# A hybrid token mixer on one Trainium2 core: the upper weight part times both token parts in one 512-column matmul

## The chip, the core and the metric

The kernel runs on one core of one Trainium2 chip. Its engines work side by side, each on its own queue of instructions in program order: PE (TensorE, matmuls and transposes), DVE (VectorE), ACT (ScalarE), POOL (GpSimd), and SP (SyncE), which here issues most DMAs. The metric is the device time of one execution in microseconds, lower is better.

## What is computed

A block of 256 tokens behind 16 learned meta tokens (272 columns) is normalised and multiplied with one wide matrix `w_in` (2048 x 18568); three recurrent mixers (A: HGRN2, B: mLSTM, C: RWKV-7) work on slices of that product; their outputs are multiplied with `w_br`, gated, summed, multiplied with `w_out`, added to the input and normalised.

```python
xn = rmsnorm(h, norm_g[l])                       # h: 16 meta tokens, then x
(a_q, a_f, a_i, a_z, b_q, b_k, b_v, b_o, b_ig, b_fg, b_z,
 c_r, c_k, c_v, c_wd, c_ad, c_z, g_a, g_b, g_c) = split_cols(xn @ w_in[l])
y_a = hgrn2_mixer(a_q, a_f, a_i, a_z, ...)
y_b = mlstm_mixer(b_q, b_k, b_v, b_o, b_ig, b_fg, b_z, ...)
y_c = rwkv7_mixer(c_r, c_k, c_v, c_wd, c_ad, c_z, ...)
merged = (jax.nn.sigmoid(g_a) * (y_a @ w_br[l, 0])
          + jax.nn.sigmoid(g_b) * (y_b @ w_br[l, 1])
          + jax.nn.sigmoid(g_c) * (y_c @ w_br[l, 2]))
h = h + merged @ w_out[l]
return rmsnorm(h, final_norm_g)[:, N_META:]
```

All of it is float32. What matters for the change is `xn @ w_in`, and that the outputs `a_q`, `a_z`, `b_o`, `b_z` and `c_z` are needed for the 256 real tokens alone.

## The kernel before, in words

**Products in two parts.** A float32 product is made of three faster ones. Tokens and weights are each cut into an upper part (rounded to the format `F32R`) and a lower part (what the rounding left): `xH`, `xL`, and `wh`, `wl`. The product is `wh*xH + wh*xL + wl*xH`, all summed in one PSUM bank. The tokens are cut once at the start. The weights come by DMA in units of 4 row tiles x 256 columns (or 2 x 512) into `raw` (four buffers); ACT casts a unit to `wh`, DVE subtracts to get `wl` (three buffers each; class `Stream`, lines 334 to 375).

**Blocks.** `proj` (line 405) enters one block per 256 output columns of `w_in`; `gemm` (line 392) runs it: 16 row tiles x 2 halves `j` of 128 output channels x 3 products, 96 matmuls, each with weights as the stationary operand and 256 to 272 token columns streaming (`unit`, line 379). When a block's 96 matmuls are done, an evacuation function works on each `j`: tanh on ACT and a multiply on DVE (`silu2_evac`, line 409), tanh alone (`o_evac`, line 957), and others. PSUM has four banks `gp` for blocks, and a block uses two of them.

**Order.** Blocks run as C0 (K, V, Z), B0 (Q, K, V, O, Z, V, O, Z), C1, B1, C2, A0, A1, C3, A2, A3 (a digit is a group; C has four groups of R, K, V, Z; A has four of F, Q, I, Z). Beside them run the recurrent parts, `c_scan` (line 508), `b_scan` and `a_scan` (line 1140), as generators. A planner (class `Order`) keeps a clock of its own for PE, ACT and DVE, charges every instruction a price, and after each half unit starts the scan steps that its clock finds ready; the tile framework then arranges the instructions of each engine by its own estimate of when they become ready. Where a scan has small matmuls, they lie between the block's big ones.

**The C scan.** Each `c_scan` ends in a serial part of five chunks (line 733). A chunk is a round trip of PE, DVE and ACT, three times: matmul `cbank<-UV,SC`, copies to `cX`; matmul `cbank<-cX,Vm`, copies to `UV`; matmul `cbank<-UV,BT`, the new state `cS`, copies to `UV` for the next chunk. Before the chunks come 31 steps of a triangular inverse on DVE (`Ltmp` and `LV`, line 657), a copy `LT`, DMAs through DRAM into `Vm` and `VT`, and the matmuls `cbank<-VT,SC` and `cbank<-Vm,ZT`.

**After the projections** (line 1367): for B, then C, then A, four blocks of gate columns of `w_in` alternate with four blocks of `w_br`, 512 columns wide. Here the tokens are stationary and the weights stream: `gp<-wh,xH` and so on, 96 matmuls per gate block, then 48 of `gp<-wh,yHB` and its kind. `yHB` and `yLB` are the two parts of B's output, cut in `split` (line 1371). They lie in the pool `late`, which `l_setup` (line 1342) opens after closing the pool of `c_scan`; the two share memory.

```python
    def l_setup():
        od.finish(cst["prev"]["scan"])
        cst["ctx"].close()
        lp = ctx.enter_context(tc.tile_pool(name="late", bufs=1, side="right"))
```

Of the kernel before, what the change touches and what calls it, by code (L numbers as in the profile page):

```python
# [10 lines left out]
F32R = mybir.dt.float32r  # L11
# [3 lines left out]
ALU = mybir.AluOpType  # L15
AX = mybir.AxisListType

P = 128
D = 2048
KT = D // P  # L20
NMETA = 16
SEQ = 256
T = NMETA + SEQ
UK = 4
# [126 lines left out]
def kernel(  # L151
# [29 lines left out]
    od = Order()  # L181
    V = Priced(nc.vector, "dve", od, tc)
    S = Priced(nc.scalar, "act", od, tc)

    def mm(o, lhsT, rhs, start, stop):
        nc.tensor.matmul(o, lhsT, rhs, start=start, stop=stop)  # L186
        n = 1
        for d in rhs.shape[1:]:
            n *= d
        od.cost("pe", max(n, 256) / 2400 + 0.003 if lhsT.dtype == F32R else max(4 * n / 2400, 0.04 if lhsT.shape[1] <= 32 else 0.1))  # L190
# [10 lines left out]
    xnp = ctx.enter_context(tc.tile_pool(name="xnp", bufs=1))  # L201
# [19 lines left out]
    def wx(shape, name, dt=F32):  # L221
        return ev.tile(shape, dt, name=name, tag="wx", bufs=6)
# [111 lines left out]
    class Stream:  # L334
# [5 lines left out]
        def add(self, src, kts):  # L340
            uk = min(UK, 1024 // src.shape[2])
            for u in range(kts // uk):
                self.todo.append(src[:, u * uk:(u + 1) * uk, :])
# [33 lines left out]
    ws = Stream()  # L377

    def unit(h, l, u, kts, ps, aH, aL, t0, n, js):
        for k in range(UK):  # L380
            kk = u * UK + k
            rh = aH[:, kk, t0:t0 + n]
            mm(ps, h[:, k, js], rh, start=kk == 0, stop=False)
            mm(ps, h[:, k, js], aL[:, kk, t0:t0 + n], start=False, stop=False)
            mm(ps, l[:, k, js], rh, start=False, stop=kk == kts - 1)

    def apart(f):
        saved, od.ready = od.ready, od.clk["pe"]
        f()
        od.ready = saved  # L390

    def gemm(m, aH, aL, kts, t0, n, evac):
        nt = m // P
        ps = [gps.tile([P, 512], F32, name="gp", tag="g") for _ in range(nt)]
        for u in range(kts // UK):
            h, l = ws.next()
            for j in range(nt):
                unit(h, l, u, kts, ps[j][:, 0:n], aH, aL, t0, n, slice(j * P, (j + 1) * P))
                od.pump()
        for j in range(nt):  # L400
            apart(lambda: evac(j, ps[j][:, 0:n]))

    blocks = []

    def proj(c0, m, t0, evac, before=None, after=None):
        ws_src = win[:, :, c0:c0 + m]
        blocks.append((ws_src, KT, lambda: gemm(m, xH, xL, KT, t0, T - t0, evac), before, after))

    def silu2_evac(dst, off=0):
        def f(j, ps):  # L410
            n = ps.shape[-1]
            o = dst()[:, j, off:off + n]
            S.activation(out=o, in_=ps, func=AF.Tanh, scale=0.5)
            V.scalar_tensor_tensor(out=o, in0=o, scalar=1.0, in1=ps, op0=ALU.add, op1=ALU.mult)
        return f

    def copy_evac(dst):
        def f(j, ps):
            S.copy(out=dst()[:, j, :], in_=ps)
        return f  # L420

    xH = xnp.tile([P, KT, T], F32R, name="xH", tag="xa")
    xL = xnp.tile([P, KT, T], F32R, name="xL", tag="xb")
    WDH = [const.tile([P, T], F32R, name=f"WDH{i}") for i in range(2)]
    WDL = [const.tile([P, T], F32R, name=f"WDL{i}") for i in range(2)]

# [33 lines left out]
    def c_group(g):  # L460
# [23 lines left out]
        if g == 0:  # L484
            alloc()
        else:
            proj(C_R + c0, 256, NMETA - 2, sh("R", 0, NMETA - 2), before=lambda: (od.finish(prev["scan"]), alloc(),
                                                          nc.gpsimd.memset(st["R"][:, :, 0:NMETA - 2], 0.0)))
        proj(C_K + c0, 256, 0, sh("K", 8))
        proj(C_V + c0, 256, 0, sh("V", 16), after=begin)  # L490
        proj(C_Z + c0, 256, NMETA, silu2_evac(lambda: st["Z"]), before=zalloc, after=zdone)
        cst["prev"] = st
        return st
# [431 lines left out]
    def b_group(g):  # L925
        st = {}
        T0 = NMETA - 4

        def alloc():
            if bst.get("last"):  # L930
                od.finish(bst["last"])
            st["Q"] = ev.tile([P, 2, T], F32, name="bQ", tag="x1")
            st["K"] = ev.tile([P, 2, T], F32, name="bK", tag="x2")

        proj(B_Q + 256 * g, 256, T0, conv_evac(lambda: st["Q"], 2 * g, T0), before=alloc)
        proj(B_K + 256 * g, 256, 0, conv_evac(lambda: st["K"], 4 + 2 * g, 0))
        for hh in range(2):
            b_head(g, hh, st)

    def b_head(g, hh, st):  # L940
        h = 2 * g + hh
        c0 = 256 * h
        hs = {"z": False}

        def valloc():
            hs["V"] = ev.tile([P, 2, T], F32, name="bV", tag="x3")

        def begin():
            od.finish(bst.get("gates"))
            od.finish(bst.get("last"))  # L950
            bst["last"] = od.start(b_scan(h, hh, st, hs), 1)

        def oalloc():
            hs["O"] = ev.tile([P, 2, SEQ], F32, name="bO", tag="x5")
            hs["Z"] = ev.tile([P, 2, SEQ], F32, name="bZ", tag="x4", bufs=2)

        def o_evac(j, ps):
            S.activation(out=hs["O"][:, j, :], in_=ps, func=AF.Tanh, scale=0.5)

        def zdone():  # L960
            hs["z"] = True

        proj(B_V + c0, 256, 0, copy_evac(lambda: hs["V"]), before=valloc, after=begin)
        proj(B_O + c0, 256, NMETA, o_evac, before=oalloc)
        proj(B_Z + c0, 256, NMETA, silu2_evac(lambda: hs["Z"]), after=zdone)
# [138 lines left out]
    def a_group(g):  # L1104
# [29 lines left out]
        flag = lambda n: (lambda: st.__setitem__(n, True))  # L1134
        proj(A_F + c0, 256, 0, f_evac, before=alloc)
        proj(A_Q + c0, 256, NMETA, silu2_evac(lambda: st["Q"], NMETA), after=begin)
        proj(A_I + c0, 256, 0, copy_evac(lambda: st["V"]), before=valloc, after=flag("v"))
        proj(A_Z + c0, 256, NMETA, silu2_evac(lambda: st["Z"]), before=zalloc, after=flag("z"))
# [199 lines left out]
    late = {}  # L1338
# [94 lines left out]
        late["x2"] = xs  # L1433

    def merge_begin(jbs):
        late["mH"] = xnp.tile([P, KT, SEQ], F32R, name="mH", tag="xa")
        late["mL"] = xnp.tile([P, KT, SEQ], F32R, name="mL", tag="xb")
        late["merge"] = od.start(merge(jbs), 0)

    def merge(jbs):  # L1440

        for jb in jbs:
            for q in range(2):
                yield "pe"
                kk = (WB // P) * jb + 2 * q
                ps = cbank()
                pv = ps.rearrange("p (c t) -> p c t", c=2)
                for c in range(2):
                    for i in range(2):
                        transpose(pv[:, c, i * P:(i + 1) * P], late["m"][jb][:, i, (2 * q + c) * P:(2 * q + c + 1) * P], ident)  # L1450
                S.copy(out=late["mH"][:, kk:kk + 2, :], in_=pv)
                V.tensor_tensor(out=late["mL"][:, kk:kk + 2, :], in0=pv, in1=late["mH"][:, kk:kk + 2, :].bitcast(F32),
                                op=ALU.subtract)
# [81 lines left out]
    for u in range(KT // UK):  # L1535
        h, l = ws.next()
        unit(h, l, u, KT, gw[0][:, 0:T], xH, xL, 0, T, slice(0, P))
        h, l = ws.next()
# [11 lines left out]
    for i, a in enumerate((rwkv_w_up, rwkv_a_up)):  # L1550
        for c in range(2):
            t = wx([P, 512], "wup")
# [19 lines left out]
    for i in range(2):  # L1572
        hs = slice(64 * i, 64 * i + 64)
# [40 lines left out]
    mH, mL = late["mH"], late["mL"]  # L1614
# [23 lines left out]
    for n, (c0, m) in enumerate(outs):  # L1638
        ps = [gps.tile([P, 512], F32, name="gp", tag="g") for _ in range(2)]
        us = KT * m // 1024  # L1640
        if n < len(outs) - 1:
            for u in range(us):
                h, l = ws.next()
# [11 lines left out]
        for i in range(2):  # L1655
# [6 lines left out]
            for q, (c0, c1) in enumerate(((0, 512), (512, 896), (896, 1536), (1536, 2048))):  # L1662
                a = hres[i][:, c0:c1]
# [35 lines left out]
```

## Time and profile before

| | |
|---|---|
| time, median of 3 runs | 1235.43 us (1233.78 to 1237.32) |
| the profiled execution's own time | 1238.05 us |
| its span, first to last instruction | 1236.3 us |
| busy: PE, DVE, ACT, POOL | 1210.1, 878.7, 665.7, 57.2 us |
| projections of `w_in` until the last block A3 Z | about 20 to 722 us |
| gate blocks, `w_br`, `w_out` | 722 us to the end |

A row of the profile's groups names engine, operation, output and inputs, their shapes, the count, the busy time and the mean duration of one, then the engine's idle time ahead of them and what ended it. Matmuls are pipelined: the duration shown for one is longer than the time until the next may start, so that spacing is read from start times or from a long piece of the chain divided by its count. In the chain and in the timeline consecutive instructions of a kind are merged, with their count. For fp32 operands that are not cut, PE shows each matmul twice.

### The profile page before, as it was taken

To read this page: it belongs to the slowest core of one execution; us is meant where nothing else is said; L and a number is where in the kernel's file an instruction comes from. 1 tells how busy PE (TensorE), PEld (TensorE's weight loads), DVE (VectorE), ACT (ScalarE), POOL (GpSimd) and SP (SyncE) were. 2 spreads that over 40 slices of the span, in tenths; PEclk is the share of its full clock that TensorE was granted. 3 is DMA by queue.
4 is the path that set the end of the run, shared out by engine and by line. 5 is a ranking of instruction groups with operands and counts; after the bars stand their busy time and mean duration, and the time that the engine had idled before them with its cause. 6 is when DMAs were issued, how large, how long until landed. Compare 5 with 4: busy or idle time off the path is not lost.

```text
span 1236.3 us, 23074 instructions
## 1 busy us (share of the span) xinstructions
PE 1210.1 (98%) x9226; PEld 1106.3 (89%) x9226; DVE 878.7 (71%) x1489; ACT 665.7 (54%) x1032; POOL 57.2 (5%) x167
## 2 busy tenths in 40 slices
PE   7999999999999999999999999999999999999997
PEld 6999999999999999989999978888888888888887
DVE  5778897687985799995889986644555555556554
ACT  5764445564445764756764757544444444445444
POOL 3100000000041000000000000000000000000000
PEclk8999999999999999999999999999999999999999
DMA  8646555455563564554554454666766676665563
GB/s 211 186 142 175 159 156 137 137 168 157 157 178 103 154 163 139 154 154 116 150 169 130 139 164 135 205 189 191 231 191 193 198 219 198 196 190 171 193 196 120
DMA packets 173124, 207.43 MB, mean 168 GB/s; under 512 B 22395, under 2 KB 127224, under 8 KB 172632
## 3 DMA queue, kind: packets, MB, share of 16 engines
q1 hardware_dynamic: 172104, 202.73, 56.1%
q0 software_dynamic: 880, 3.22, 0.8%
q8 instruction: 72, 1.18, 0.4%
q14 instruction: 36, 0.29, 0.1%
q10 hardware_dynamic: 32, 0.01, 0.0%
HBM read 202.19 MB, written 3.74 MB: 167 GB/s over the span
## 4 chain that ended last, share of the span: by engine, by line
PE 84%; DVE 9%; ACT 3%; issue 2%; DMA 1%; SPq 0%; ACTq 0%; DVEq 0%
PE gp L186 76%; PE cbank L186 4%; DVE wl L127 3%; PE bank L186 3%; ACT wh L127 1%; DVE Ltmp L127 1%; DMA xt<-in_x_dram 1%; DVE LV L127 1%; PE cbank L193 1%; PE bank L193 1%; DVE UV L127 0%; DVE aM L127 0%; DVE aY L127 0%; ACT L127 0%; DVE aW L127 0%
## 5 line engine op out<-in xcount | busy, mean ns | idle before, releaser
L127 DVE TENSOR_TENSOR wl<-raw,wh 128x1024 fp32r<-128x1024 f32 (+1 forms) x370 | 449.1, 1215 | 242.2 <-ACT wh L127 240.7
L127 ACT CAST wh<-raw 128x1024 fp32r<-128x1024 f32 (+1 forms) x370 | 386.5, 1045 | 387.3 <-PE gp L186 358.2
L186 PE MATMUL gp<-xH,wh 128*128 128x272 f32 (+3 forms) x1552 | 449.5, 290 | 0.2 <-ACT xH L127 0.2
L186 PE MATMUL gp<-xH,wl 128*128 128x272 f32 (+3 forms) x1552 | 445.1, 287 | 1.6 <-DVE wl L127 1.6
L186 PE MATMUL gp<-xL,wh 128*128 128x272 f32 (+3 forms) x1552 | 444.8, 287 | 0.0
L186 PEld LDWEIGHTS gp<-xH,wl 128*128 128x128 f32 x1552 | 293.4, 189 | 3.0 <-DVE wl L127 2.7
L186 PEld LDWEIGHTS gp<-xH,wh 128*128 128x128 f32 x1552 | 293.7, 189 | 2.2 <-ACT xH L127 0.5
L186 PEld LDWEIGHTS gp<-xL,wh 128*128 128x128 f32 x1552 | 293.5, 189 | 0.8 <-DVE xL L127 0.2
L186 PE MATMUL gp<-wh,xH 128*128 128x512 f32 x384 | 150.7, 392 | 0.0
L186 PE MATMUL gp<-wh,xL 128*128 128x512 f32 x384 | 150.5, 392 | 0.0
L186 PE MATMUL gp<-wl,xH 128*128 128x512 f32 x384 | 150.2, 391 | 0.0
L186 PEld LDWEIGHTS gp<-wh,xL 128*128 128x128 f32 x384 | 72.1, 188 | 15.4
L186 PEld LDWEIGHTS gp<-wl,xH 128*128 128x128 f32 x384 | 72.2, 188 | 15.2
L186 PEld LDWEIGHTS gp<-wh,xH 128*128 128x128 f32 x384 | 72.1, 188 | 15.0
L186 PE MATMUL gp<-wh,mH 128*128 128x512 f32 (+1 forms) x144 | 51.1, 355 | 0.0
L186 PE MATMUL gp<-wl,mH 128*128 128x512 f32 (+1 forms) x144 | 51.0, 354 | 0.0
L186 PE MATMUL gp<-wh,mL 128*128 128x512 f32 (+1 forms) x144 | 50.9, 354 | 0.0
L127 DVE TENSOR_TENSOR LV<-LV,Ltmp 40x31 f32<-40x31 f32 (+15 forms) x124 | 41.0, 330 | 2.6
L127 DVE TENSOR_TENSOR Ltmp<-LU,LV 40x31 f32<-40x31 f32 (+15 forms) x124 | 41.0, 331 | 2.4
L186 PEld LDWEIGHTS gp<-wh,mL 128*128 128x128 f32 x144 | 27.2, 189 | 3.7
L186 PEld LDWEIGHTS gp<-wl,mH 128*128 128x128 f32 x144 | 27.2, 189 | 3.7
L186 PEld LDWEIGHTS gp<-wh,mH 128*128 128x128 f32 x144 | 27.2, 189 | 3.7
(412 smaller groups left out, 1476.5 us busy)
## 6 DMA issues: line engine op xcount, KB each, us to landing
raw<-in_w_in_dram SPq DMA_DIRECT2D x288, 512.0 KB, 3.6
raw<-in_w_br_dram SPq DMA_DIRECT2D x48, 512.0 KB, 3.8
raw<-in_w_out_dram SPq DMA_DIRECT2D x32, 512.0 KB, 3.6
hres<-in_x_dram POOLq DMA_DIRECT2D x2, 1024.0 KB, 5.8
raw<-in_w_in_dram SPq DMA_DIRECT2D x4, 256.0 KB, 2.9
fg<-in_final_norm_g_dram POOLq DMA_DIRECT2D x1, 1024.0 KB, 5.3
out_dram<-hres SPq DMA_DIRECT2D x4, 256.0 KB, 2.6
xt<-in_x_dram SPq DMA_DIRECT2D x3, 320.0 KB, 6.8
```

The costliest lines, as they stand in the source:

```text
L127: r = f(*a, **k)
L186: nc.tensor.matmul(o, lhsT, rhs, start=start, stop=stop)
L193: nc.tensor.transpose(o, a, i)
```

## The change

In blocks whose outputs are the 256 real tokens alone (`n == SEQ`), the two products with `wh` become one: the moving operand is the 256 columns of `xH` and the 256 of `xL`, and the result fills a whole bank of 512, its first half `wh*xH`, its second `wh*xL`. The product `wl*xH` adds into the first half. From the second row tile on, `wl*xH` is issued ahead of the joined one. At the end ACT copies the second half into the tile that the evacuation will write, DVE adds it to the first half in PSUM, and the evacuation goes on as before. These blocks are C Z, B O, B Z, A Q and A Z, four of each, 20 in all. So that one access pattern reaches both parts, `xH` and `xL` become the two halves of one tile `xHL`; the merged activations `mH` and `mL`, which take that memory later, become one tile too.

```diff
-    def gemm(m, aH, aL, kts, t0, n, evac):
+    def gemm(m, t0, evac):
         nt = m // P
+        n = T - t0
         ps = [gps.tile([P, 512], F32, name="gp", tag="g") for _ in range(nt)]
+        if n == SEQ:
+            for u in range(KT // UK):
+                h, l = ws.next()
+                for j in range(nt):
+                    js = slice(j * P, (j + 1) * P)
+                    for k in range(UK):
+                        kk = u * UK + k
+                        two = ((ps[j].rearrange("p (a t) -> p a t", a=2), h, xHL[:, :, kk, t0:T]),
+                               (ps[j][:, 0:n], l, xH[:, kk, t0:T]))
+                        for i, (o, w, a) in enumerate(two if kk == 0 else two[::-1]):
+                            mm(o, w[:, k, js], a, start=kk == i == 0, stop=kk == KT - 1 and i == 1)
+                    od.pump()
+
+            def add(j):
+                o = evac.dst(j)
+                S.copy(out=o, in_=ps[j][:, n:2 * n])
+                V.tensor_tensor(out=ps[j][:, 0:n], in0=ps[j][:, 0:n], in1=o, op=ALU.add)
+                evac(j, ps[j][:, 0:n])
+
+            for j in range(nt):
+                apart(lambda: add(j))
+            return
...
-    xH = xnp.tile([P, KT, T], F32R, name="xH", tag="xa")
-    xL = xnp.tile([P, KT, T], F32R, name="xL", tag="xb")
+    xHL = xnp.tile([P, 2, KT, T], F32R, name="xHL", tag="x")
+    xH, xL = xHL[:, 0], xHL[:, 1]
...
+        o_evac.dst = lambda j: hs["O"][:, j, :]
```

The planner prices the joined matmul, the copies and the adds as it does all others, so the arrangement of other instructions moves as well. Three places show it.

The first is PE in the fourth `c_scan` (group 3), chunk after chunk of its serial part, while the first gate block of B runs. Before, a late chunk of it stands among the gate block's matmuls (`gp` rows):

```order
L186 MATMUL cbank<-UV,SC 128x128 x2
L186 MATMUL gp<-wh,xL 128x512
L186 MATMUL gp<-wh,xH 128x512
L186 MATMUL gp<-wl,xH 128x512
L186 MATMUL gp<-wh,xL 128x512
L186 MATMUL cbank<-cX,Vm 128x64 x2
L186 MATMUL gp<-wh,xH 128x512
L186 MATMUL gp<-wl,xH 128x512
L186 MATMUL gp<-wh,xL 128x512
L186 MATMUL gp<-wh,xH 128x512
L186 MATMUL gp<-wl,xH 128x512
L186 MATMUL cbank<-UV,BT 64x64 x4
```

With the change, the same scan's last two chunks:

```order
L186 MATMUL cbank<-UV,SC 128x128 x2
L186 MATMUL cbank<-cX,Vm 128x64 x2
L186 MATMUL cbank<-UV,BT 64x64 x4
L186 MATMUL cbank<-SC,UV 64x64 x2
L186 MATMUL cbank<-RA,Zs 64x64 x2
L186 MATMUL cbank<-SC,UV 64x64 x2
L186 MATMUL cbank<-RA,Zs 64x64 x2
L186 MATMUL cbank<-UV,SC 128x128 x2
L186 MATMUL cbank<-cX,Vm 128x64 x2
L186 MATMUL cbank<-SC,UV 64x16 x2
L186 MATMUL cbank<-RA,Zs 64x16 x2
L186 MATMUL cbank<-SC,UV 64x16 x2
```

Before, `cbank<-VT,SC`, which opens this part, stands behind 3 of the gate block's 96 matmuls, and the colsums `cSL,bonesR` that follow the chunks behind 83. With the change `cbank<-VT,SC` stands behind 80 of them, chunk 0 between numbers 85 and 96, and chunks 1 to 4 behind all 96.

The second is PE at the end of that scan. Before, the colsums are followed by the rest of the gate block:

```order
L186 MATMUL cbank<-cSL,bonesR 128x256
L186 MATMUL cbank<-cSH,bonesR 128x256
L186 MATMUL cbank<-cSL,bonesR 128x256
L186 MATMUL cbank<-cSH,bonesR 128x256
L186 MATMUL gp<-wh,xL 128x512
L186 MATMUL gp<-wh,xH 128x512
```

With the change they are followed by the first block of `w_br`:

```order
L186 MATMUL cbank<-cSL,bonesR 128x256
L186 MATMUL cbank<-cSH,bonesR 128x256
L186 MATMUL cbank<-cSL,bonesR 128x256
L186 MATMUL cbank<-cSH,bonesR 128x256
L186 MATMUL gp<-wh,yHB 128x512
L186 MATMUL gp<-wl,yHB 128x512
```

The third is DVE at the end of the last projection block, A3 Z (`aZ`), where the fourth `a_scan` (`aE`, `aW`) and the inverse of the fourth `c_scan` (`Ltmp`, `LV`) run. Before:

```order
L127 TENSOR_TENSOR aE<-aC 128x136x2 x2
L127 TENSOR_TENSOR wl<-raw,wh 128x1024
L127 TENSOR_TENSOR aW_9531<-aE,aK 128x136x2
L127 TENSOR_TENSOR aW_9531<-aE,aQ 128x136x2
L127 SCALAR_TENSOR_TENSOR aZ<-aZ,gp 128x256 x2
L127 TENSOR_TENSOR wl<-raw,wh 128x1024
L127 TENSOR_TENSOR aMM<-bank,am 128x320
```

With the change:

```order
L127 TENSOR_TENSOR gp<-gp,aZ 128x256
L127 TENSOR_TENSOR LV<-LV,Ltmp 40x5x27
L127 TENSOR_TENSOR gp<-gp,aZ 128x256
L127 TENSOR_TENSOR Ltmp<-LU,LV 40x112
L127 TENSOR_TENSOR wl<-raw,wh 128x1024
L127 TENSOR_TENSOR LV<-LV,Ltmp 40x4x28
L127 SCALAR_TENSOR_TENSOR aZ<-aZ,gp 128x256 x2
L127 TENSOR_TENSOR Ltmp<-LU,LV 40x87
L127 TENSOR_TENSOR aE<-aC 128x68x4
```

Before, `LV`, its copy `LT` and the last `aW` of `a_scan` stand ahead of the evacuation of A3 Z. With the change the last four steps of `LV`, `LT`, four rows of `aE` and four of `aW` stand behind it.

## Rows read from the trace of the kernel before

**Rows 1.** The page: the span, and busy time, share and instructions of each engine.

```profile
span 1236.3 us, 23074 instructions
PE 1210.1 (98%) x9226; PEld 1106.3 (89%) x9226; DVE 878.7 (71%) x1489; ACT 665.7 (54%) x1032; POOL 57.2 (5%) x167
```

**Rows 2.** The page: the chain that ended last, by engine.

```profile
PE 84%; DVE 9%; ACT 3%; issue 2%; DMA 1%; SPq 0%; ACTq 0%; DVEq 0%
```

**Rows 3.** Groups by form: PE in the 256-column blocks and in a gate block.

```profile
L186 PE MATMUL gp<-xH,wh 128*128 128x256 f32 x640 | 182.1, 285 | 0.0
L186 PE MATMUL gp<-xH,wl 128*128 128x256 f32 x640 | 180.0, 281 | 1.6 <-DVE wl L127 1.6
L186 PE MATMUL gp<-xL,wh 128*128 128x256 f32 x640 | 179.5, 280 | 0.0
L186 PE MATMUL gp<-wh,xH 128*128 128x512 f32 x384 | 150.7, 392 | 0.0
```

**Rows 4.** The chain in order of time: start us, us, what, with its count.

```profile
601.27 7.09 PE gp L186 x60
...
770.89 355.09 PE gp L186 x1560
```

**Rows 5.** Groups by form: ACT and DVE instructions of 256 columns that read PSUM.

```profile
L127 ACT COPY avt<-bank 128x256 f32<-128x256 f32 x4 | 1.5, 384 | 0.0
L127 DVE TENSOR_TENSOR SC<-cbank,cmask 128x256 f32<-128x256 f32 x32 | 11.6, 415 | 0.0
```

**Rows 6.** Who waited for whom: engine, line, released by: us, times, longest.

```profile
ACT wh L127 <- PE gp L186: 358.2, 234, 5.0
```

**Rows 7.** The same for PE alone.

```profile
PE gp L186 <- DVE wl L127: 1.6, 4, 0.7
```

**Rows 8.** Windows: start:end, length, busy of PE, PEld, DVE, ACT, POOL, clock, DMA.

```profile
450.00:500.00 50.00, 48.79 (x576) 47.18 (x575) 45.57 (x108) 24.85 (x40) 0.32 (x2) 1.00 0.53 151
500.00:550.00 50.00, 48.64 (x610) 46.88 (x610) 47.04 (x100) 34.10 (x61) 0.41 (x2) 1.00 0.57 162
650.00:700.00 50.00, 48.52 (x569) 47.58 (x569) 48.13 (x114) 29.04 (x51) 0.13 (x1) 1.00 0.51 143
```

**Rows 9.** Windows: end of projections to the first matmul with B's output.

```profile
722.10:762.20 40.10, 38.03 (x422) 30.07 (x421) 26.20 (x58) 24.54 (x58) 3.59 (x8) 1.00 0.35 108
```

**Rows 10.** Timeline of the fourth C scan's serial part: start us, us, engine, operation.

```profile
723.63 0.47 PE L186 MATMUL cbank<-VT,SC 32*32 32x32 f32 x17
...
728.06 0.71 PE L186 MATMUL cbank<-UV,SC 128*128 128x128 f32 x4
...
734.80 0.62 PE L186 MATMUL cbank<-UV,SC 128*128 128x128 f32 x4
...
741.53 0.68 PE L186 MATMUL cbank<-UV,SC 128*128 128x128 f32 x4
...
751.59 0.60 PE L186 MATMUL cbank<-UV,SC 128*128 128x128 f32 x4
...
755.07 0.19 ACT L127 COPY cY<-cbank 128x32 f32<-128x32 f32 x1 [0.82 <-PE cbank L186]
755.15 0.62 ACT L127 CAST yHB<-yB 128x512 fp32r<-128x512 f32 x1
...
762.19 0.48 PE L186 MATMUL gp<-wh,yHB 128*128 128x512 f32 x1
```

**Rows 11.** Timeline: one chunk of the third C scan, from matmul to matmul.

```profile
558.42 0.68 PE L186 MATMUL cbank<-UV,SC 128*128 128x128 f32 x4
...
563.03 0.71 PE L186 MATMUL cbank<-UV,SC 128*128 128x128 f32 x4
```

**Rows 12.** Groups by form: ACT reading a gate block's bank.

```profile
L127 ACT ACTIVATE sg<-gp 128x512 f32<-128x512 f32 x24 | 14.4, 600 | 11.9 <-PE gp L186 11.9
```

**Rows 13.** Groups by form: PE in the late part of the A scans, four scans together.

```profile
L186 PE MATMUL bank<-ATT,avt 128*128 128x256 f32 x16 | 5.1, 399 | 0.0
```

**Rows 14.** Timeline: small matmuls of the fourth A scan, merged, with their count.

```profile
723.05 0.65 PE L186 MATMUL bank<-aW 128*32 128x32 f32 x46
```

More of the change, by code (lines that the diff above doesn't have):

```diff
@@ L390, in apart @@
         od.ready = saved
-    def gemm(m, aH, aL, kts, t0, n, evac):
+    def gemm(m, t0, evac):
         nt = m // P
+        n = T - t0
         ps = [gps.tile([P, 512], F32, name="gp", tag="g") for _ in range(nt)]
-        for u in range(kts // UK):
+        if n == SEQ:
[18 more added lines that the diff above has]
+            return
+        for u in range(KT // UK):
             h, l = ws.next()
             for j in range(nt):
-                unit(h, l, u, kts, ps[j][:, 0:n], aH, aL, t0, n, slice(j * P, (j + 1) * P))
+                unit(h, l, u, KT, ps[j][:, 0:n], xH, xL, t0, n, slice(j * P, (j + 1) * P))
                 od.pump()
@@ L406, in proj @@
         ws_src = win[:, :, c0:c0 + m]
-        blocks.append((ws_src, KT, lambda: gemm(m, xH, xL, KT, t0, T - t0, evac), before, after))
+        blocks.append((ws_src, KT, lambda: gemm(m, t0, evac), before, after))
     def silu2_evac(dst, off=0):
@@ L414, in f @@
             V.scalar_tensor_tensor(out=o, in0=o, scalar=1.0, in1=ps, op0=ALU.add, op1=ALU.mult)
+        f.dst = lambda j: dst()[:, j, off:off + SEQ]
         return f
@@ L1435, in merge_begin @@
     def merge_begin(jbs):
-        late["mH"] = xnp.tile([P, KT, SEQ], F32R, name="mH", tag="xa")
-        late["mL"] = xnp.tile([P, KT, SEQ], F32R, name="mL", tag="xb")
+        mHL = xnp.tile([P, 2, KT, T], F32R, name="mHL", tag="x")
+        late["mH"], late["mL"] = (mHL[:, i].rearrange("p k t -> p (k t)")[:, 0:KT * SEQ].rearrange("p (k t) -> p k t", t=SEQ)
+                                  for i in range(2))
         late["merge"] = od.start(merge(jbs), 0)
```

## The prediction

> **What bounds the kernel now.** I read the page first: PE is busy 98% of the span, DVE 71%, ACT 54% [rows 1]. The chain that ended last says the same, 84% of it PE [rows 2]. A busy PE need not be a PE at its peak, so the next question is how close the big matmuls follow each other. The groups show 285 ns for one of 256 columns and 392 ns for one of 512 [rows 3], but they overlap. The chain gives the spacing: 60 matmuls of 256 columns (in block C3 Z) in 7.09 us are 118.2 ns each, and 1560 of 512 in 355.09 us are 227.6 ns each [rows 4]. So two matmuls of 256 take 236.4 ns where one of 512 takes 227.6. The reader is to see that nearly all the time goes with the columns, and that only 8.8 ns hang on the instruction. Then I looked at who waits: PE waits for the lower weight part for 1.6 us in all [rows 7], ACT's weight casts wait for PE for 358 us [rows 6]. PE sets the pace nearly everywhere. DVE is near full where A and C scans run together (45.6 to 48.1 us of 50) [rows 8]. Last I read the one stretch in which a scan's serial part has little other work beside it, from the end of the projections to the first matmul with B's output: 40.1 us [rows 9, 10].
>
> **The change part by part.**
>
> *Joined matmuls.* 20 blocks x 16 row tiles x 2 halves are 640 triples, as the counts of 640 say [rows 3]. A triple was 3 x 118.2 = 354.6 ns and becomes 227.6 + 118.2 = 345.8 ns. 640 x 8.8 ns = **5.6 us less** on PE, which is the path. Column counts are the same, 768 per triple. The trace has no moving operand in two pieces, so this term has bounds: nothing, if the two pieces stream as two matmuls do; more than 5.6 is excluded by the columns, which stay (the two rows give 0.427 ns for each and 8.8 ns for the instruction). I take 5.6, since the 512-column row is the nearest form.
>
> On this the Trainium skill has a rule that speaks against the change: its page "TensorE: Matmul & The Clock Gate", section "Back-to-back issue gap", gives an isolated warm gap of N/2.4 + 2.5 ns, so a matmul saved would be worth 2.5 ns. By that 640 of them give 1.6 us, and the sum below would end 4 us higher. The chain's rows don't agree with it: 118.2 ns for 256 columns where the rule has 109.2.
>
> *640 weight loads less.* They overlap with matmuls now and cost nothing; their cover is the matmul before them, and it becomes longer.
>
> *Copy and add at the end of a block.* 40 copies on ACT at 0.384 us (15.4 us) and 40 adds on DVE at 0.415 us (16.6 us) [rows 5]. Per half the evacuation becomes a round trip ACT, DVE, ACT, DVE, with up to 0.8 us more; behind the waiting tanh stand ACT's next weight casts. PE doesn't need the bank: the next block has the other two, for 11 us. What covers the casts is ACT's wait for PE, 358 us in all, 1.5 us at each of its 234 times [rows 6]. I cost it at nothing on ACT. Without that cover it would be 40 x 0.8 = 32 us, which no row suggests.
>
> *DVE in the dense stretches.* The eight A blocks add 8 x 0.83 = 6.6 us to a DVE that has 2 to 4 us free in 50 [rows 8]. But the changed order moves about as much off DVE until the projections are over: four `LV` steps, `LT`, four `aE` and four `aW` now stand behind the last evacuation. Also `wl` is now the first operand of a unit instead of the third, so PE needs it 2 x 118 ns earlier; at the 4 waits that PE has for it [rows 7] that is 1 us. Between 0 and 6.6 + 1 I take **1.0 us more**, near the lower end, because those waits are short now.
>
> *The fourth C scan's serial part.* This is the large term, and it isn't in the diff but in the order. Before, the scan's chunks lie between the gate block's matmuls, which fill every wait. Now 80 of the 96 gate matmuls come first, and chunks 1 to 4 stand behind all of them with nothing large between. The next big matmul is the one with `yHB`. That tile lies in memory that this scan must leave first: its first cast started at 755.15, right when the last chunk was over, at 755.07 [rows 10]. So nothing can fill the gap. From the end of the projections, worked out for the changed order:
> - 80 gate matmuls x 227.6 ns, 18.2 us, and all 88 small A matmuls of the pairwise part, which PE shows twice, 176 x 14 ns [rows 14], 2.5 us: `VT,SC` at 20.7.
> - From there to chunk 1 the trace has 734.80 - 723.63 = 11.2 us [rows 10], with 23 gate matmuls in it; now there are 16, and a wait or two less. I take 8.5: chunk 1 at 29.2.
> - Chunks 1 to 3: 6.7 us where an A scan competes on ACT and DVE (734.80 to 741.53) [rows 10], 4.6 us at best [rows 11]. With the A scan's end in the same rows I take 5.3 each: 45.1.
> - Chunk 4 to its last copy, 751.59 to 755.07, 3.4 us [rows 10]: 48.5.
> - ACT then has two `sg` at 0.6 [rows 12], two squares and the first cast at 0.62 [rows 10]: 3.1 us, first `yHB` matmul at **51.6**.
>
> Before it was 40.1 [rows 9]. Of the 11.5 us between them, work that only changed places comes off: the first 52 small A matmuls, which stood ahead of 722 (1.5 us), and the A scan's `ATT` matmuls (5.1 us for four scans, so 1.3) [rows 13] with four colsums (0.5), which stood behind 762. That leaves **8.2 us more**. Bounds: with 7.5 and 4.6 instead of 8.5 and 5.3 it is 5.1; with 11.2 and 6.7 it is 15.1.
>
> *Other moves.* The first three C scans have their chunks between projection matmuls before and after, a few matmuls later: nothing. SP's queue passes the scan's DMAs to `Vm` and `VT` later, with weight loads behind them; four buffers of `raw` cover that, and the 20.7 us ahead of `VT,SC` cover their landing. POOL's copies to `Zs` follow the chunks. One tile for `xH` and `xL` is written once per part as before, and `mH`, `mL` come when both were free anyway: nothing.
>
> **Sum.** -5.6 + 1.0 + 8.2 = +3.6 us against the profiled execution's 1238.05. The median of the runs stands 2.6 below that, so the forecast on it is 1235.4 + 3.6 = **1239.0**. About 0.3% (3.7 us) is what a measurement of this kernel can tell from no change; the forecast lies on that line.
>
> **Rivals.**
> 1. *The tail is covered after all* (faster). Place: between the 96th gate matmul and `yHB`. If chunks run at their least and A's work in the gaps is worth more than I took off, the tail costs nothing and the time is 1235.4 - 5.6 + 1.0 = 1230.8. It decides when the stretch from the end of the projections to `yHB` stays under 48.0 us (43.4 and the 4.6 won elsewhere); below that the kernel is no slower. For it: PE's work is less in all and only waits can cost. Against it: eleven round trips follow each other with no big matmul in reach.
> 2. *The tail is worse.* ACT and DVE have the A scan's copies and roots between a chunk's steps, in their order. At 11.2 and 6.7 us the tail costs 15.1 instead of 8.2: 1246. The 6.7 us chunks are for it, the 4.6 us chunk against.
> 3. *Two pieces stream as two.* The joined matmul takes 236 ns or more and nothing is saved: 1235.4 + 1.0 + 8.2 = 1244.6. For it, that no row has such an operand; against it, that 512 columns in one piece cost less than two of 256. The Trainium skill's gap rule named above would lead near this.
> 4. *DVE becomes the bound in the A groups.* Its 6.6 us go to PE through late `wl`: 1235.4 - 5.6 + 7.6 + 8.2 = 1245.6. DVE's 48 of 50 us speak for it; that PE waits 1.6 us for `wl` in all, against.
>
> **Chances.** The forecast's case 0.52, with its own range of 1236 to 1243 from the bounds of the tail, half of it on each side of the line; rival 1 0.20 (of that 0.15 clear of the line); rival 2 0.13; rival 3 0.08; rival 4 0.07. Slower by over 0.3%: 0.26 + 0.13 + 0.08 + 0.07 = 0.54. Faster: 0.15. Within: 0.31. The range reaches to rival 1 and to rival 2: 1231 to 1246.
>
> **What would show it.** Right: PE at about 346 ns per triple in the 20 blocks; 40 copies near 0.38 and 40 adds near 0.42 us with no new wait of PE behind them; between the gate block and the first `yHB` matmul some 20 us in which PE has only chunk matmuls and waits for `cX`, `UV` and `cS`; that stretch, from the end of the projections, near 52 us. Wrong: a stretch near 40 us, `wl` waits of several us, or 512-column matmuls spaced well over 230 ns.

## The result and the profile after

| | before | after |
|---|---|---|
| median of 4 runs, same chip | 1234.71 us (1233.78 to 1237.32) | 1253.75 us (1251.47 to 1255.08) |
| ratio, 95% interval | | 1.0151 (1.0131 to 1.0170) |
| from the start of block C0 K to the end of the projections | 677.8 us | 679.3 us |
| end of the projections to the first `yHB` matmul | 40.0 us | 57.5 us |
| first `yHB` matmul to the last matmul | 465.8 us | 465.7 us |

The kernel became 19.0 us slower, 7.8 us beyond the forecast range. The lower three rows are read from start times on PE. They begin at C0 K because the load ahead of it took 40.5 to 44.3 us in the executions profiled here, whatever the kernel. Nearly the whole loss lies in one stretch, and the projections, where 640 matmuls fewer run, gained nothing.

The page of after, span, PE and granted clock in 40 slices (about 31 us each); it answers to [rows 1]:

```profile
span 1253.4 us, 21866 instructions
PE 1216.2 (97%) x8586; PEld 1080.3 (86%) x8586; DVE 887.4 (71%) x1529; ACT 675.4 (54%) x1072; POOL 53.0 (4%) x167
...
PEclk8999999999999999989999996999999999999999
```

PE has fewer instructions and yet more busy time. What changed stands in the last line: an 8 in the middle and a 6 behind it, slices in which the granted clock was lower. Before, no slice but the first was under 9.

Windows of after: the stretch of [rows 9] as a whole, its three parts, and what follows. Columns as in [rows 8].

```profile
721.93:779.40 57.47, 46.69 (x541) 37.38 (x540) 37.70 (x88) 32.21 (x71) 2.39 (x8) 0.87 0.38 109
721.93:746.80 24.87, 24.04 (x328) 18.93 (x326) 23.53 (x54) 14.72 (x25) 0.00 (x0) 1.00 0.65 184
746.80:763.80 17.00, 14.43 (x160) 11.46 (x153) 6.59 (x17) 9.87 (x30) 1.44 (x5) 1.00 0.34 99
763.80:779.40 15.60, 8.22 (x62) 6.99 (x62) 7.57 (x17) 7.62 (x17) 0.95 (x4) 0.50 0.00 1
779.40:784.00 4.60, 4.60 (x12) 3.63 (x12) 3.17 (x5) 2.86 (x5) 0.57 (x1) 0.50 0.02 4
```

In the first part gate matmuls fill PE. In the second PE is busy 14.43 of 17 us. In the third the clock is 0.50, that is 1.2 GHz; PE is busy half the time, DMA does nothing, and it stays so for 4.6 us of `yHB` matmuls (12 in 4.6 us). Before, the whole stretch had 1.00 and 37.97 busy of 40.04.

Timeline of the serial part in after, as in [rows 10]; a bracket gives idle time ahead and its releaser:

```profile
743.58 0.71 PE L186 MATMUL cbank<-VT,SC 32*32 32x32 f32 x32
...
746.84 0.71 PE L186 MATMUL cbank<-UV,SC 128*128 128x128 f32 x4
...
752.05 0.71 PE L186 MATMUL cbank<-UV,SC 128*128 128x128 f32 x4
...
758.31 0.67 PE L186 MATMUL cbank<-UV,SC 128*128 128x128 f32 x4
...
763.85 1.13 PE L186 MATMUL cbank<-UV,SC 128*128 128x128 f32 x4
765.83 1.12 PE L186 MATMUL cbank<-cX,Vm 128*128 128x64 f32 x4 [0.85 <-ACT cX L127]
767.62 0.70 PE L186 MATMUL cbank<-UV,BT 128*64 128x64 f32 x8 [0.67 <-ACT UV L127]
...
770.39 1.22 PE L186 MATMUL cbank<-UV,SC 128*128 128x128 f32 x4 [1.21 <-ACT UV L127]
...
775.54 0.19 ACT L127 COPY cY<-cbank 128x32 f32<-128x32 f32 x1 [1.14 <-PE cbank L186]
...
778.41 0.55 PE L186 MATMUL cbank<-cSL,bonesR 128*128 128x256 f32 x1 [2.92 <-DVE cSL L127]
...
779.40 0.63 PE L186 MATMUL gp<-wh,yHB 128*128 128x512 f32 x1
```

Small matmul groups of 0.67 to 0.71 us take 1.13 to 1.22 from chunk 3 on. PE waits 0.7 to 1.2 us at a step of the round trip. Chunk 1 (from 752.05) and chunk 2 (from 758.31) ran ahead of the fall, at full clock, and took 6.3 and 5.5 us.

Groups by form in after: the joined matmul (512 columns) and its partner, then one of the new copies and adds (8 each per kind of block; the others differ by 0.01 us):

```profile
L186 PE MATMUL gp<-xHL,wh 128*128 128x512 f32 x640 | 226.0, 394 | 0.2
L186 PE MATMUL gp<-xHL,wl 128*128 128x256 f32 x640 | 174.4, 282 | 3.9 <-DVE wl L127 3.9
L127 DVE TENSOR_TENSOR gp<-gp,bZ 128x256 f32<-128x256 f32 x8 | 3.4, 425 | 0.1
L127 ACT COPY bZ<-gp 128x256 f32<-128x256 f32 x8 | 3.0, 374 | 5.4 <-PE gp L186 4.9
```

Copies of 0.37 and adds of 0.42 us are as forecast [rows 5]. PE's waits for `wl` grew from 1.6 us [rows 7] to 3.9.

### The profile page after: what moved, and what is told of

Its sections match the earlier page's. It is cut to its first block, busy times and chain, and to the rows that moved or that the text cites. A ratio compares the mean times of both kernels' runs of the same rounds, so it can differ in the third digit from the quotient of the medians.

```text
span 1253.4 us, 21866 instructions
## 1 busy us (share of the span) xinstructions
PE 1216.2 (97%) x8586; PEld 1080.3 (86%) x8586; DVE 887.4 (71%) x1529; ACT 675.4 (54%) x1072; POOL 53.0 (4%) x167
## 4 chain that ended last, share of the span: by engine, by line
PE 85%; DVE 9%; ACT 3%; issue 1%; DMA 1%; SPq 0%; ACTq 0%; DVEq 0%
PE gp L186 76%; PE cbank L186 5%; DVE wl L127 3%; PE bank L186 2%; ACT wh L127 1%; DMA xt<-in_x_dram 1%; PE cbank L193 1%; DVE Ltmp L127 1%; DVE LV L127 1%; PE bank L193 1%; DVE aM L127 0%; DVE aW L127 0%; DVE aE L127 0%; ACT SC L127 0%; ACT ATT L127 0%
## 5 line engine op out<-in xcount | busy, mean ns | idle before, releaser
L186 PE MATMUL gp<-xHL,wh 128*128 128x272 f32 (+3 forms) x2464 | 581.5, 319 | 0.4 <-ACT xHL L127 0.2
L186 PE MATMUL gp<-xHL,wl 128*128 128x272 f32 (+3 forms) x1552 | 439.7, 288 | 3.9 <-DVE wl L127 3.9
L186 PEld LDWEIGHTS gp<-xHL,wh 128*128 128x128 f32 x2464 | 407.8, 190 | 26.5 <-DVE cV L127 0.6
L186 PEld LDWEIGHTS gp<-xHL,wl 128*128 128x128 f32 x1552 | 293.3, 189 | 7.7 <-DVE wl L127 5.2
L186 PE MATMUL gp<-wh,xH 128*128 128x512 f32 x256 | 99.6, 389 | 0.0
L186 PE MATMUL gp<-wh,xL 128*128 128x512 f32 x256 | 99.6, 389 | 0.0
L186 PE MATMUL gp<-wh,xHL 128*128 128x512 f32 x256 | 81.4, 396 | 0.0
L186 PE MATMUL gp<-wh,mHL 128*128 128x512 f32 (+1 forms) x288 | 77.3, 354 | 0.0
L186 PEld LDWEIGHTS gp<-wh,mHL 128*128 128x128 f32 x288 | 51.2, 189 | 7.4
L186 PE MATMUL gp<-wl,mHL 128*128 128x512 f32 (+1 forms) x144 | 50.9, 354 | 0.0
```

## The experiments

The theory after the result (A): the place of the fourth C scan's serial part, behind the gate block, costs the time, not the joined blocks as such. Its rivals are named in each expectation. Each run was timed beside the kernel before on the same chip; runs on different chips are compared by their ratios.

| run | time, us | ratio to before, 95% |
|---|---|---|
| e1, change, CAP 4.0 | 1241.38 | 1.0055 (1.0036 to 1.0073) |
| e2, change, copies and adds unpriced | 1235.93 | 1.0012 (1.0004 to 1.0021) |
| e3, before, late scan | 1248.53 | 1.0115 (1.0101 to 1.0128) |
| e4, change, taken apart | 1247.47 | 1.0112 (1.0095 to 1.0128) |
| e5, change, gaps filled | 1247.35 | 1.0111 (1.0096 to 1.0127) |
| e6, change, two blocks exchanged | 1237.67 | 1.0029 (1.0020 to 1.0038) |
| e7, unpriced and exchanged | 1231.45 | 0.9984 (0.9975 to 0.9993) |
| e8, before, exchanged | 1233.09 | 0.9993 (0.9984 to 1.0002) |
| e9, e7 taken apart | 1238.24 | 1.0041 (1.0028 to 1.0054) |
| e10, exchanged, no copies and adds | 1230.95 | 0.9981 (0.9972 to 0.9990) |
| e11, e7 with AHEAD 4.0 | 1234.56 | 1.0011 (1.0002 to 1.0019) |
| e12, e7 with AHEAD 4.5 | 1240.97 | 1.0058 (1.0045 to 1.0071) |
| e13, e7 with `wl` behind | 1236.53 | 1.0016 (1.0007 to 1.0026) |

### The order without the joined matmul, and the reverse

e3 is the kernel before with one planner number altered:

```diff
-    AHEAD = 3.5
+    AHEAD = 2.5
```

> The kernel before, nothing joined, with AHEAD 2.5 instead of 3.5 in the planner: VT,SC stands behind 74 of the 96 gate matmuls, the chunks behind 78, 94, 96, 96, 96, much as in the changed kernel. Theory A: the stretch from the end of the projections to the first yHB matmul becomes 50 to 57 us instead of 40.1, with a granted clock below 1.00 at its end, and the time 1245 to 1253 without any joined matmul. Rival B: within 4 us of the kernel before, 1232 to 1239.

Measured: +13.7 us, and this window of e3 from the end of the projections to `yHB`:

```profile
719.65:774.21 54.56, 46.28 (x537) 37.22 (x535) 37.05 (x86) 30.79 (x69) 2.37 (x8) 0.87 0.40 115
```

Nothing is joined here, and length, PE's busy time and the clock of 0.87 are nearly those of after. The late place alone makes most of the loss, 13.7 of 19.0 us; rival B falls.

e1 keeps the whole change and alters the planner's other number:

```diff
-    CAP = 5.0
+    CAP = 4.0
```

> The changed kernel with one number of the planner altered: CAP, by how much its ACT and DVE clocks may run ahead of PE's, 4.0 instead of 5.0. Every product, copy and add of the change stays; only the order moves: VT,SC of the fourth C scan stands behind 2 matmuls of the first gate block instead of 80, its five chunks behind 8, 27, 48, 56 and 69 (kernel before: 3; 7, 26, 44, 58, 70). Theory A (the loss is the place of that scan's serial part, the joined matmul itself saves about 5 us): the stretch from the end of the projections to the first yHB matmul comes back to 40 to 42 us, the granted clock stays at 1.00 there, and the time is 1229 to 1234. Rival B (joined blocks cost by themselves, through the operand in two pieces, the copies or the adds): 1245 to 1254 whatever the order. Rival C (both): 1236 to 1244.

The stretch came back as theory A said (41.9 us, clock 1.00), the time did not: 1241.4, in the range of rival C. From C0 K to the end of the projections e1 took 677.8 us where e2, below, took 673.5. Of these 4.3 us 1.5 are 104 small A matmuls that stand behind the projections in e2 (14 ns each); scan steps released at other times may account for the rest, which is not shown. The six runs lay between 1237.1 and 1245.1, with a mean granted clock of 0.995 in the fastest and 0.989 in the slowest.

e2 keeps all work and takes only the prices away:

```diff
-                S.copy(out=o, in_=ps[j][:, n:2 * n])
-                V.tensor_tensor(out=ps[j][:, 0:n], in0=ps[j][:, 0:n], in1=o, op=ALU.add)
+                nc.scalar.copy(out=o, in_=ps[j][:, n:2 * n])
+                nc.vector.tensor_tensor(out=ps[j][:, 0:n], in0=ps[j][:, 0:n], in1=o, op=ALU.add)
```

> The changed kernel with the 40 copies and 40 adds left out of the planner's prices (they run all the same). VT,SC then stands behind 41 gate matmuls, the chunks behind 45, 60, 73, 85 and 92. Theory A: chunks stay covered by gate matmuls except for the last few us; the last chunk comes 22 x 0.23 = 5 us later than in the kernel before, of which about 2 to 4 show; stretch 42 to 44 us, time 1231 to 1236. Rival B: 1245 to 1254, as for the change. Rival C: 1238 to 1244.

The same instructions in another order are 17 us faster than the change. The stretch is 44.5 us, and the projections are 4.3 us shorter than before. So copies, adds and joined matmuls together lose little by running: e2 is 1.5 us slower than the kernel before, with a stretch that is 4.5 us longer. The rest is the order.

### The granted clock

e5 adds matmuls whose result nobody reads, in the gaps of chunks 1 to 4:

```diff
+        if kts == 8 and "warm" not in late:
+            late["warm"] = True
+            for k in range(90):
+                nc.tensor.matmul(ps[1][:, 0:256], onesR, xH[:, k % KT, NMETA:T], start=True, stop=True)
```

> The changed kernel with 90 extra matmuls of 256 columns (onesR by xH, 118 ns each at full clock, 10.6 us in all) into the bank that the first block of w_br will fill from scratch later; their result is never read. In PE's order they stand, 5 to 14 at a place, exactly in the gaps of chunks 1 to 4 of the fourth C scan and behind them, where the changed kernel's PE waits and its granted clock falls from 1.00 to 0.50. Theory A (the fall of the clock to 1.2 GHz is part of the cost: nine groups of small matmuls take 1.1 to 1.2 us instead of 0.62 to 0.7, and the first yHB matmuls are spaced 0.43 instead of 0.23 us): clock 1.00 throughout, the stretch from the end of the projections to yHB 52 to 55 us instead of 57.5, time 1247 to 1251. Rival B (only the round trips between the engines cost, the clock is a symptom): stretch 57 to 59, time 1253 to 1256.

Windows of e5, the same three parts as in after:

```profile
718.39:743.30 24.91, 24.06 (x328) 18.92 (x326) 23.55 (x54) 14.74 (x25) 0.00 (x0) 1.00 0.63 188
743.30:758.37 15.07, 14.84 (x152) 12.64 (x147) 6.17 (x16) 5.84 (x16) 1.78 (x6) 1.00 0.34 105
758.37:769.51 11.14, 11.14 (x132) 10.22 (x132) 3.10 (x9) 5.09 (x14) 0.58 (x2) 1.00 0.01 1
```

The last two chunks on its timeline, with the added matmuls between the steps:

```profile
757.87 0.69 PE L186 MATMUL cbank<-UV,SC 128*128 128x128 f32 x4
...
758.33 1.07 PE L1391 MATMUL gp<-xHL,onesR 128*128 128x256 f32 x7
...
759.30 0.66 PE L186 MATMUL cbank<-cX,Vm 128*128 128x64 f32 x4
...
762.36 0.69 PE L186 MATMUL cbank<-UV,SC 128*128 128x128 f32 x4
```

PE does 10.6 us more work and the kernel is faster. The first part is equal to 0.04 us (24.87 and 24.91). Then the clock stays at 1.00, groups stay at 0.7 us, chunks 1 to 3 take 5.0, 4.5 and 4.5 us instead of 6.3, 5.5 and 6.5, and the stretch is 51.1 us instead of 57.5, below the range of theory A. In the medians the two kernels are 0.40% apart (5 us).

The clock is not the only thing that differs there, though. The added matmuls also moved the fourth A scan's late work. In after it lies between the chunks, and in chunk 1 six of its copies on ACT stand ahead of the chunk's copy to `UV`:

```profile
754.73 1.35 ACT L127 COPY ATT<-bank 32x192 f32<-32x192 f32 x6 [1.28 <-PE bank L186]
755.94 0.66 PE L193 MATMUL bank<-ident,aV 128*128 128x128 f32 x4 [0.78 <-ACT ATT L127]
756.10 0.26 ACT L127 COPY UV<-cbank 64x128 f32<-64x128 f32 x1
```

In e5 the chunk's copy does not wait for them, and they stand behind the scan and the first `yHB` matmul (769.50):

```profile
751.09 0.26 ACT L127 COPY UV<-cbank 64x128 f32<-64x128 f32 x1 [1.32 <-DVE UV L127]
...
771.61 0.29 ACT L127 COPY ATT<-bank 32x192 f32<-32x192 f32 x1
772.46 1.88 ACT L127 COPY ATT<-bank 32x128 f32<-32x128 f32 x9
```

So 2.3 of the 6.4 us, those of chunks 1 and 2, were lost at full clock. From chunk 3 on the gain is 3.9 us, with clock and A's work both different. An estimate of the clock's part goes by the matmul groups of chunks 3 and 4 and the colsums, which take 0.25 to 0.53 us longer in after: about 3 us together. e5 does not separate the two causes further.

The same pair shows a first fall, in the third C scan, where the orders of PE, ACT and DVE agree. Windows of 5 us there, of after:

```profile
550.00:555.00 5.00, 3.38 (x80) 2.95 (x79) 4.93 (x11) 3.95 (x8) 0.12 (x1) 1.00 0.43 111
555.00:560.00 5.00, 4.88 (x24) 4.36 (x23) 2.78 (x6) 3.80 (x10) 0.00 (x0) 0.57 0.34 102
560.00:565.00 5.00, 4.90 (x41) 4.51 (x41) 1.84 (x6) 1.88 (x4) 1.02 (x4) 0.75 0.37 105
```

In e5 the same instructions start 0.98 us earlier. Its windows, shifted by that:

```profile
549.02:554.02 5.00, 3.38 (x80) 2.96 (x80) 4.93 (x11) 3.95 (x8) 0.12 (x1) 1.00 0.39 111
554.02:559.02 5.00, 4.57 (x46) 4.13 (x46) 3.48 (x10) 4.37 (x12) 0.56 (x3) 1.00 0.31 102
559.02:564.02 5.00, 4.90 (x56) 4.46 (x55) 2.30 (x6) 1.62 (x4) 0.47 (x2) 1.00 0.54 156
```

Both executions have PE busy 3.38 of 5 us with the same 80 matmuls, in one the clock then falls, in the other not. Behind the fall (0.50 for 6.8 us, by the trace's record of the granted clock) the same matmul starts at 563.08 in after and at 559.51 in e5: the distance grew from 0.98 to 3.57 us. Here the clock is the only difference found, and its price is 2.6 us. e6, below, has the same order in the projections and fell there for half as long, 3.4 us. From C0 K to the end of the projections after took 679.3 us, e6 677.6 and e5 676.6.

### Cover in place of speed

e6, e7 and e8 exchange two blocks, so that the second gate block of B stands between the scan and `yHB`. e6 is the change so edited, e7 also has the unpriced copies and adds of e2, e8 is the kernel before.

```diff
+    n = len(blocks) - 7
+    blocks[n], blocks[n + 1] = blocks[n + 1], blocks[n]
     gate_branch("C", G_C, 2, False, False, lambda: [])
```

> The changed kernel with two blocks exchanged after the projections: the second gate block of B runs ahead of the first block of w_br, so PE has 96 more matmuls of 512 columns (21.8 us) that don't need yHB. Chunks 1 to 4 of the fourth C scan then stand behind 97, 104, 118 and 130 of 192 gate matmuls. Theory A (the 17 us lost between projections and yHB are PE without work that it may do): 14 to 18 us come back, 1235 to 1240, and PE has no wait over 2 us there. Rival B (the loss is elsewhere, or the order gives it back at the next wait for yHB): above 1246.

> The run without prices for copies and adds, with the same two blocks exchanged. Theory A: its stretch to yHB was 4.5 us longer than in the kernel before; that comes back, 1230 to 1233, which would be faster than the kernel before by the worth of the joined matmuls (measured so far 0.18 us per undisturbed block, 3.6 to 4 us for 20). Rival B: the exchange gives nothing, 1235 to 1237.

> The kernel before with the same two blocks exchanged, nothing joined. In its 40.1 us stretch PE is busy 38.0, so theory A expects 0 to 2 us less, 1232.5 to 1235; the run without prices and with the exchange then stays 2 to 4 us below this one. Rival B (the exchange alone is the gain, the joined matmuls are worth nothing): both runs within 1 us of each other.

The times of all three came out as theory A expected, the distance between e7 and e8 did not (below). The stretch, now with 192 gate matmuls, as a window of e6:

```profile
719.04:785.09 66.05, 64.54 (x637) 51.46 (x636) 47.73 (x97) 43.38 (x86) 2.93 (x9) 1.00 0.50 156
```

Of e7:

```profile
714.58:780.91 66.33, 65.21 (x638) 51.25 (x636) 50.34 (x94) 44.34 (x88) 2.98 (x9) 1.00 0.49 156
```

And of e8:

```profile
718.98:782.07 63.09, 62.42 (x533) 50.22 (x532) 48.22 (x87) 44.91 (x85) 4.15 (x9) 1.00 0.45 148
```

PE is busy nearly throughout, at 1.00. The chunks are as late in e6 as in the change, and 15 us of the 19 come back. e7 is the complete version that beats the kernel before, by 0.16% (0.07 to 0.25%). Against e8 the gain is 1 us only, with intervals that overlap, so that theory A's 2 to 4 us did not come and the gain by the joined matmuls is not clear of rival B in the time alone. e7's projections are 4.3 us shorter, and 3.2 us come back in the stretch, where e7 has 104 small A matmuls more (1.5 us at 14 ns). e7's profiled execution also had the clock at 0.50 for 3.4 us in the projections, e8's did not.

### The joined matmul by itself

e4 takes it apart and keeps the rest of the change:

```diff
-                        two = ((ps[j].rearrange("p (a t) -> p a t", a=2), h, xHL[:, :, kk, t0:T]),
+                        tri = ((ps[j][:, 0:n], h, xH[:, kk, t0:T]), (ps[j][:, n:2 * n], h, xL[:, kk, t0:T]),
                                (ps[j][:, 0:n], l, xH[:, kk, t0:T]))
...
```

> The changed kernel with the joined matmul taken apart again: wh x xL goes by itself into the second half of the bank, three matmuls of 256 columns per triple; the one tile xHL, the copies, the adds and wl first stay. VT,SC stands behind 40 gate matmuls, chunks behind 45, 59, 75, 80, 94, nearly as in the run without prices. Theory A: about 5 us (640 x 8 ns) slower than that run, 1236 to 1241. Rival B1 (the operand in two pieces is what costs): as fast as the kernel before or faster, 1231 to 1236, and faster than the run without prices. Rival B2 (copies and adds cost): 1245 to 1256.

It missed theory A's range upwards: 1247.5, inside B2's. But its order is not that of e2 in the projections (687.1 us against 673.5; 104 small A matmuls more stand in them, and the clock was at 0.50 for 6.8 us against 3.4), so it doesn't settle B2; e10 does, below. e9 makes the same edit in e7.

> The run without prices and with the two blocks exchanged, but the joined matmul taken apart into two of 256 columns (wh x xL by itself into the second half of the bank); copies and adds stay. With the tail covered and the copies unpriced, what remains between this and that run is the joined matmul. Theory A (a joined matmul saves what the undisturbed block A0 Q showed, 11.33 - 11.15 = 0.18 us for 32 triples, 5.6 ns each): 640 x 5.6 = 3.6 us slower, ratio to the kernel before 1.000 to 1.003. Rival B (8.8 ns each, as predicted): 5.6 us slower, ratio 1.002 to 1.005. Rival C (nothing saved): ratio 0.997 to 0.999, equal to that run.

e9 is 0.57% (7 us) slower than e7, by the time alone nearest to rival B. The blocks say otherwise. A window of the block A0 Q, there without scan work, in after (64 matmuls and two at the edges):

```profile
438.12:449.27 11.15, 11.15 (x66) 9.78 (x65) 10.87 (x19) 9.91 (x15) 0.13 (x1) 1.00 0.56 157
```

The same block in e3, with 96:

```profile
439.39:450.72 11.33, 11.33 (x98) 11.33 (x97) 10.54 (x18) 10.69 (x16) 0.13 (x1) 1.00 0.58 170
```

32 triples differ by 0.18 us. In e7 and e9 the same block, there with scan work in it, takes 12.33 and 12.51, again 0.18. For 20 blocks that is 3.6 us. The other 3.4 of e9 are put down to the order (its `wl` waits are 5.8 us against 4.2), which no run separates.

### Copies, adds and the place of wl

e10 is e6 without copy and add:

```diff
-                S.copy(out=o, in_=ps[j][:, n:2 * n])
-                V.tensor_tensor(out=ps[j][:, 0:n], in0=ps[j][:, 0:n], in1=o, op=ALU.add)
```

> The changed kernel with the two blocks exchanged and without the 40 copies and 40 adds: the products wh x xL of the 20 blocks are left out of the result (they are still computed). VT,SC stands behind 37 gate matmuls, about as in the run without prices and with the exchange (41). Theory A (the copies and adds lie beside PE's work and cost nothing by their execution, only by what their prices do to the order): within 1.5 us of that run, 1230 to 1233. Rival B (their 40 round trips reach PE through late weight casts or the bank): 3 us or more faster, below 1228.5.

0.03% below e7, with the intervals nearly the same: to within about 1 us 40 copies and 40 adds cost nothing by running, as forecast. (The two orders are close to each other, not equal.) The edit takes their prices away too, and with those 0.48% (6 us) against e6.

e13 keeps one order of the two products in e7:

```diff
-                        for i, (o, w, a) in enumerate(two if kk == 0 else two[::-1]):
+                        for i, (o, w, a) in enumerate(two):
```

> The run without prices and with the two blocks exchanged, but wl x xH stands behind the joined matmul for every row tile, as it did in the kernel before, so PE needs the lower weight part one matmul of 512 columns (0.23 us) later. Theory A (wl is late because it is now needed first): PE's waits for wl fall from 4.2 us to about 2 to 3, and the time is 1 to 2 us below that run, ratio to the kernel before 0.996 to 0.998. Rival B (wl is late because of what else the order puts ahead of it on DVE; 0.23 us more matters little): waits of 3.5 us or more, ratio 0.9975 to 1.000.

Rival B's waits came (4.7 us), its time did not: e13 is 4 us slower than e7, and its profiled execution had the clock at 0.50 for 6.8 us in the projections against 3.4. Why the waits grew stays open; they did not fall with `wl` behind, nor without the copies and adds (4.1 us in e10).

### An earlier scan once more

e11 is e7 with this edit, e12 has 4.5 there:

```diff
-    AHEAD = 3.5
+    AHEAD = 4.0
```

> The run without prices and with the exchange, AHEAD 4.0 instead of 3.5: VT,SC behind 16 gate matmuls instead of 41, chunks behind 21, 42, 60, 73 and 80. Theory A: the tail's waits are covered by the exchanged gate block already, so an earlier serial part gains 0 to 1.5 us: 1230 to 1232. Rival (steps started earlier collide with casts and the lower weight parts in the projections, as in the run with CAP 4.0): 1233 to 1240.

> The same with AHEAD 4.5: VT,SC behind 3 gate matmuls, chunks behind 8, 30, 56, 69 and 74. Theory A: 1229.5 to 1232. Rival, as for AHEAD 4.0: 1233 to 1240, and if both are slower, the later one here more so.

The rival's times came, in the second 1 us above its range. The stretch shortens to 64.0 and 64.4 us from 66.3, but the projections grow from 673.4 us to 678.4 and 685.1. The rival's reason is shown for a part at most: PE's waits for `wl` are 4.4 and 6.4 us, in e7 4.2. Of the growth 1.5 us are the 104 small A matmuls, which are back in the projections, and some is clock: 6.8 and 10.2 us at 0.50 there, against 3.4. The rest is open. With a covered tail an earlier scan won nothing.

## Why the prediction was wrong

| term | predicted | measured |
|---|---|---|
| joined matmuls | -5.6 | -3.6 |
| DVE and `wl` | +1.0 | +3.1 in the order of the projections, +2.7 for the first fall of the clock |
| end of projections to `yHB`, ahead of the credit | 51.6 us, +11.5 | 57.5 us, +17.4 |
| credit for moved work | -3.3 | -1.5 ahead of the stretch; -0.1 behind it, where the slow clock took back the rest (estimate) |
| sum | +3.6 | +19.0 |

By place, the forecast missed by 7.6 us in the projections (expected 5.6 less, 1.0 more and 1.5 moved out of them, measured +1.5), by 5.9 in the stretch and by 1.7 behind it. Two steps failed.

**The first is the fourth C scan's serial part.** Its mechanism was right, PE without large matmuls between chunk and `yHB`, and so was its start: `VT,SC` was put at 20.7 us from the end of the projections and came at 21.7; from there to chunk 1 it was 8.5 and measured 8.5. Its latencies were too small. Chunks of 5.3 took 6.3 and 5.5 at full clock, with the A scan's copies on ACT between their steps, and 6.5 behind the fall. Chunk 4 to its last copy was put at 3.4 and took 5.2, the rest to `yHB` at 3.1 and took 3.9, both at half clock. So 2.2 of the 5.9 us were lost at full clock and 3.7 at half, where A's work stands in between too. What the step left out is that PE, with only small matmuls and waits, loses its clock: to 1.2 GHz from about 764 to 784 us, behind a part in which it was busy 14.4 of 17 us. The trace of before had the clock at 1.00 throughout that stretch, so no row priced this; but the text foresaw some 20 us with "only chunk matmuls and waits" and did not ask what the clock does then.

**The second is the term for DVE and `wl`, 1.0 us.** It priced the running of copies and adds, and that costs nothing (e10). Their planner prices move other steps: e5, with the change's order and no fall of the clock, took 676.6 us in the projections, e2, with the same instructions there in another order, 673.5 (and would have taken less without its 3.4 us at 0.50). So at least 3.1 us of the saving went to the order, and 2.7 to the first fall of the clock, which the text did not foresee at all. PE's waits for `wl` there are 3.8 us in both, so late casts are not the difference. Two waits for scan steps, which after and e5 have and e2 does not, come to 3.4 us (of e5; who waited, for whom, us in total, times, longest):

```profile
PE bank L186 <- DVE aKL L127: 1.8, 1, 1.8
PE cbank L186 <- ACT ZT L127: 1.6, 1, 1.6
```

With all terms, from C0 K to the last matmul: -4.3 (projections in e2, joined matmuls and moved work) + 3.1 + 2.7 + 17.4 - 0.1 = 18.8 us.

**The credit of 3.3 us came, and was taken back in part.** Of it 104 small A matmuls, 1.5 us, did leave the projections. The other 1.8 should have shown behind `yHB`, where A's last matmuls and the colsums no longer stand; but there 465.7 us stand against 465.8. In just that part lie the 12 `yHB` matmuls at 1.2 GHz, spaced 0.43 us instead of 0.23: about 2.3 us more, by estimate. That the two cancel is argued, not tested.

**The joined term was over by 2 us.** The step was "the 512-column row is the nearest form". With 118.0 ns for the `wl` matmul, the block of 11.15 us gives 230.4 ns for the joined one, not 227.6: a triple saves 5.6 ns and not 8.8. The Trainium skill's 2.5 ns ("TensorE: Matmul & The Clock Gate", "Back-to-back issue gap") would have been 1.6 us by estimate; the measured 3.6 lies between. The row itself [rows 4] is a mean over blocks that differ. Windows of before, each a gate block of 96 matmuls whose moving operand is one piece of 512 columns, the first of B, the second of C:

```profile
775.51:797.75 22.24, 22.24 (x97) 18.03 (x96) 15.85 (x20) 12.72 (x13) 0.00 (x0) 1.00 0.63 190
874.89:896.65 21.76, 21.76 (x97) 18.02 (x96) 13.10 (x14) 10.98 (x13) 0.54 (x1) 1.00 0.74 242
```

That is 231.7 and 226.7 ns from one matmul to the next, so 230.4 does not show that the second piece of the operand costs something.

**The rivals.** "The tail is worse" (rival 2) gave 1246, below what came. Its reason, the A scan's copies and roots between a chunk's steps, held for chunks 1 and 2; the clock came on top. Two pieces streaming as two (rival 3) is refuted by the 0.18 us per block, DVE as the bound by its copies and adds (rival 4) by e10. The tail covered after all (rival 1) did not come, but e6 shows that cover was the missing thing.

## What to carry to other kernels

When a change moves a chain of small dependent steps out of the shadow of large matmuls, price the stretch twice, at full clock and at 1.2 GHz, with the matmuls that follow it, and add what other work stands between its steps on ACT and DVE. The mend that worked here was neither a faster chain nor an earlier place for it, but one independent block of large matmuls behind it. And a cost that a planner charges can move more time than the instruction itself takes.

## What the runs showed of the hardware

- The clock fell from 1.00 to 0.50 though PE never waited more than 1.0 us at a time in the 17 us ahead, busy 14.43 of them. In e5, with 90 matmuls of 118 ns in the waits, it stayed at 1.00.
- The same order of instructions, with the same 3.38 us of 5 busy, was followed by a fall in after and by none in e5. The fall, 6.8 us at 0.50, cost 2.6 us. e1's runs of one program differ by 8 us, the slower ones with the lower mean clock.
- Matmuls with a moving operand in two pieces of 256 columns, 512 in all, are spaced 230.4 ns (after, block A0 Q). With 512 columns in one piece it is 231.7 and 226.7 ns in two gate blocks of before, so the pieces show no price of their own.
